# RWKV-7 chunk inverses: 16x16 diagonal blocks doubled twice, in place of 32x32 blocks doubled once

## The chip, the cores and the metric

The kernel runs on one core of a Trainium2 chip. The metric is the device time of one execution in microseconds (us), lower is better. Before the change three runs took 1123.34, 1129.8 and 1132.21 us; the median is 1129.8.

## The reference

One decoder layer on 512 tokens of width 1024, in float32. The token-mixing half computes one projection of the normed input, and from it two branches: an RWKV-7 scan over 16 heads of size 64, and a causal convolution of width 31 on 1024 channels. Both are gated, joined and projected back. A dense feed-forward half of width 4096 follows. The part that the change touches is the scan:

```
def step(S, inp):
    r_t, w_t, k_t, v_t, a_t, b_t = inp
    sa = jnp.einsum('bhij,bhj->bhi', S, a_t)
    S = S * w_t[:, :, None, :] + sa[..., None] * b_t[:, :, None, :] + v_t[..., None] * k_t[:, :, None, :]
    return S, jnp.einsum('bhij,bhj->bhi', S, r_t)
```

Taken over a chunk of 64 tokens, the steps inside the chunk depend on one another through a strictly lower triangular 64x64 matrix (per head and chunk). The kernel multiplies by the inverse of one minus that matrix, and so handles a chunk with a few matrix products in place of 64 steps.

## The kernel before, in words

The layer runs as one program on the five engines: PE (matrix products), DVE and POOL (vector work), ACT (activations and copies), SP (issues the DMAs). Large products are done as three passes over a high and a low part of each operand; the split of a weight tile into these parts is done on ACT and on DVE or POOL (`split`, L145), and a tile of raw weights is loaded for each projection (`wcol`, L154).

The 16 heads are handled in four quarters of four heads, that is, two pairs of heads each; a sequence of 512 tokens has 8 chunks, so a quarter has 32 chunk matrices. For a quarter these steps follow one another:

- R (`rkv_pair`, L483): projections for a pair of heads and their elementwise preparation.
- I (`products`, L547): PE forms the chunk matrices, DVE masks them into M (L567). Then DMAs write blocks of M to DRAM (L571): per pair the two diagonal 32x32 blocks and the off-diagonal one.
- V (`solve`, L580): reads the 64 diagonal 32x32 blocks of the quarter back into U (L586), two partitions to a block, one for the even and one for the odd rows of the inverse. POOL prepares X as the identity (L590, L593). 31 steps follow, each a product (L598) and a sum (L600) on DVE, each step depending on the one before. X is written to DRAM (L603).
- O (`scan_operands`, L606): transposes for the scan.
- M (`merge_inverses`, L629): reads the inverted blocks and the off-diagonal block into W (L639) and the diagonal blocks into RT (L640, L641). One transpose (L642), one product of 32x32 blocks on PE (L648), a copy (L650), a second product and four copies into RT (L652) give the off-diagonal block of the 64x64 inverse: left inverse times block times right inverse, for 32 matrices.
- S (`scan`, L655): the chunks of the quarter in order. For each chunk PE makes a first product that does not need the inverse (L669), one with the inverse RT (L680, recorded as L184), and the products for output and next state (L691, L693), with small copies on ACT and DVE between them.
- Y (`group_norm`, L707): normalises the output of the quarter.

The other steps of this phase are U and T (the convolution: projections, L732, and 30 taps per tile of 128 channels on DVE, L745), G and B (gates), N, and after the last quarter the tail (`enter_tail`, L822) with the output projection and then the feed-forward layer.

What sets the order of the work is the string ORDER (L35): it lists these steps, each with a number that lets its instructions go ahead of that many others in priority. A planner at build time orders the instructions of every engine by priority and by its own cost for each; on the chip each engine then works through its list in order, waiting on semaphores. All DMAs are issued by SP, in one list. U and W share one buffer of 4 KB per partition (tag "U" of the pool xq); X, and the scan's operands, are in the pool qp, which is closed before the tail.

Of the kernel before, what the change touches and what calls it, by code (L numbers as in the profile page):

```python
# [62 lines left out]
def tile_rwkv7_conformer(  # L63
# [389 lines left out]
    with ExitStack() as c1:  # L453
# [93 lines left out]
        def products(q, prs):  # L547

            d1 = dram.tile([3, 32, 32, 32], F32, name=f"d1_{q}")
            pcq[q] = qp.tile([C, NCHK, 4, 1], F32, tag="pcq", name=f"pcq{q}", bufs=2)  # L550
            for pr, d in enumerate(prs):
# [18 lines left out]
                for b, (s0, t0) in enumerate(((0, 0), (32, 32), (0, 32))):  # L570
                    nc.sync.dma_start(out=d1[b, pr * 16:(pr + 1) * 16].rearrange("h s t -> s h t"),  # L571
                                      in_=Mf[s0:s0 + 32, :, t0:t0 + 32])
# [5 lines left out]
            return d1  # L578

        def solve(q, d1):  # L580

            d2 = dram.tile([2, 32, 32, 32], F32, name=f"d2_{q}")
            U = xq.tile([P, 32, 32], F32, tag="U", name=f"U{q}")
            d1f = d1[0:2].rearrange("b h s t -> (b h) (s t)")
            for par in range(2):
                nc.sync.dma_start(out=U[64 * par:64 * par + 64].rearrange("p s t -> p (s t)"), in_=d1f)  # L586

            X = qp.tile([P, 16, 32], F32, tag="X", name=f"X{q}")
            tmp = qp.tile([P, 136], F32, tag="tmp", name=f"tmp{q}")
            G.memset(X, 0.0)  # L590
            for par in (0, 1):
                xv = X[64 * par:64 * par + 64]
                G.affine_select(out=xv, in_=xv, compare_op=ALU.not_equal, fill=1.0, base=-par,  # L593
                                pattern=[[-2, 16], [1, 32]], channel_multiplier=0)
            for s in range(31):
                n, m = s // 2 + 1, 31 - s
                tv = tmp[:, 0:n * m].rearrange("p (a b) -> p a b", b=m)
                V.tensor_tensor(tv, X[:, 0:n, s:s + 1].to_broadcast([P, n, m]),  # L598
                                U[:, s:s + 1, s + 1:32].to_broadcast([P, n, m]), op=ALU.mult)
                V.tensor_tensor(X[:, 0:n, s + 1:32], X[:, 0:n, s + 1:32], tv, op=ALU.add)  # L600
            d2v = d2.rearrange("b h (i two) t -> two (b h) i t", two=2)
            for par in range(2):
                nc.sync.dma_start(out=d2v[par], in_=X[64 * par:64 * par + 64])  # L603
            return d1, d2
# [24 lines left out]
        def merge_inverses(q, d1, d2):  # L629
# [4 lines left out]
            W = xq.tile([P, 4, 8, 32], F32, tag="U", name=f"W{q}")  # L634
            lay, grp = "h i t -> i h t", "(g x) i t -> g i x t"
            for g in range(4):
                gs = slice(32 * g, 32 * g + 32)
                for m, src in enumerate((d1[2], d2[0], d2[1])):
                    nc.sync.dma_start(out=W[gs, m], in_=src[8 * g:8 * g + 8].rearrange(lay))  # L639
            nc.sync.dma_start(out=RT[64:96, :, 0:32], in_=d2[0].rearrange(lay))  # L640
            nc.sync.dma_start(out=RT[96:128, :, 32:64], in_=d2[1].rearrange(lay))  # L641
            V.transpose(W[:, 3].rearrange("p x t -> p (x t)"), W[:, 1].rearrange("p x t -> p (x t)"))  # L642
            for a, b, dst in ((0, 3, 1), (1, 2, None)):
                px = pq.tile([P, 8, 32], F32, tag="q", name=f"px{q}{a}")
                for x_ in range(8):
                    for g in range(4):
                        gs = slice(32 * g, 32 * g + 32)
                        PE.matmul(px[gs, x_, :], W[gs, a, x_], W[gs, b, x_], start=True, stop=True)  # L648
                if dst is not None:
                    S.copy(W[:, dst], px)  # L650
# [459 lines left out]
```

## Time and profile before

| what | value |
|---|---|
| median of three runs | 1129.8 us |
| the profiled execution's own time | 1131.94 us |
| its span | 1130.2 us |
| PE busy | 1023.5 us, 91% of the span |
| DVE busy | 790.1 us, 70% |
| ACT busy | 479.1 us, 42% |
| POOL busy | 198.2 us, 18% |
| mean granted PE clock over the span | 0.953 of full speed |

An engine counts as busy while one of its instructions runs; matrix products overlap, so a busy PE is not a PE at its peak. The span is that of the profiled execution, and the time beside it is what the same execution took as a whole. The order of the phases in the span: until about 60 us input, norm and modulation, until about 600 us the projections, the scan and the convolution, until about 780 us the output projection and its surroundings, and then the feed-forward layer.

### The profile page before, as it was taken

Reading aid. Unit: us, or ns where it says so; the run is one execution under the profiler, and the core shown is the slowest. Engines: PE = TensorE matmul, PEld = TensorE weight load, DVE = VectorE, ACT = ScalarE, POOL = GpSimd, SP = SyncE. Lnnn points to the kernel's source line nnn. Section 1 sums busy time; section 2 is a strip of 40 time slices with the busy share of each in tenths; the row PEclk is TensorE's granted clock in tenths of the full one; section 3 lists DMA queues with packets and bytes.
Section 4 is the critical chain, followed back from the end, with each engine's and each line's share of the span. In section 5 each row is a group of like instructions: output and inputs, shape, how many; then the busy total and the mean of one; then the engine's idle time right before and its main releaser. Section 6 shows DMA issues by size and latency. Waiting matters only on the chain.

```text
span 1130.2 us, 16757 instructions
## 1 busy us (share of the span) xinstructions
PE 1023.5 (91%) x6037; PEld 792.5 (70%) x6037; DVE 790.1 (70%) x1622; ACT 479.1 (42%) x912; POOL 198.2 (18%) x191
## 2 busy tenths in 40 slices
PE   2999889889899789996997999899999999999995
PEld 1777666656677666665665767688888888888874
DVE  3859999969958997989455787585445445445557
ACT  5546445374644356534343433264323323423432
POOL 1123042222422533221121121200000000000002
PEclk9999999989999989996798999999999999999998
DMA  9622332331343234324257686731223323333332
GB/s 313 181 72 87 88 100 73 54 92 48 104 117 94 86 95 83 85 66 110 94 162 234 224 273 217 232 104 38 84 93 95 101 94 94 95 93 100 96 103 74
DMA packets 184605, 131.34 MB, mean 116 GB/s; under 512 B 49945, under 2 KB 152779, under 8 KB 184523
## 3 DMA queue, kind: packets, MB, share of 16 engines
q1 hardware_dynamic: 184523, 130.28, 39.1%
q8 instruction: 47, 0.77, 0.3%
q14 instruction: 35, 0.29, 0.1%
HBM read 116.61 MB, written 13.63 MB: 115 GB/s over the span
## 4 chain that ended last, share of the span: by engine, by line
PE 43%; DVE 16%; DMA 5%; issue 3%; ACT 3%; POOL 1%; SPq 0%; DVEq 0%; ACTq 0%; POOLq 0%
PE ps_fi L174 5%; PE ps_fi L175 5%; PE ps_fi L176 5%; DVE cz L745 5%; PE acc_fo L1005 4%; PE acc_fo L1004 4%; PE acc_fo L1003 4%; DMA ar<-in_ada_w_dram 2%; DVE tmp L598 1%; DVE aacc L217 1%; PE ps_ga L175 1%; PE ps_ga L176 1%; PE ps_ga L174 1%; DVE X L600 1%; PE pr L669 1%
## 5 line engine op out<-in xcount | busy, mean ns | idle before, releaser
L745 DVE SCALAR_TENSOR_TENSOR cz<-gl,cw,cz 128x512 f32<-128x512 f32 x240 | 200.8, 837 | 3.9 <-ACT cz L743 1.2
L151 DVE TENSOR_TENSOR lo_fo<-raw_fo,hi_fo 128x512 fp32r<-128x512 f32 x64 | 44.2, 691 | 92.1 <-ACT hi_fo L150 91.9
L175 PE MATMUL ps_fi<-hl,hi_fi 128*128 128x512 f32 (+1 forms) x288 | 105.6, 367 | 0.0
L176 PE MATMUL ps_fi<-hh,lo_fi 128*128 128x512 f32 (+1 forms) x288 | 105.3, 367 | 0.0
L174 PE MATMUL ps_fi<-hh,hi_fi 128*128 128x512 f32 (+1 forms) x288 | 105.0, 367 | 0.0
L1003 PE MATMUL acc_fo<-hi_fo,fh 128*128 128x512 f32 x256 | 101.3, 396 | 0.8 <-DVE t_fo L1010 0.8
L1004 PE MATMUL acc_fo<-lo_fo,fh 128*128 128x512 f32 x256 | 101.2, 395 | 0.0
L1005 PE MATMUL acc_fo<-hi_fo,fl 128*128 128x512 f32 x256 | 101.2, 395 | 0.0
L150 ACT CAST hi_fo<-raw_fo 128x512 fp32r<-128x512 f32 x64 | 39.7, 621 | 110.6 <-PE acc_fo L1005 87.8
L151 DVE TENSOR_TENSOR lo_fi<-raw_fi,hi_fi 128x512 fp32r<-128x512 f32 x64 | 43.8, 690 | 52.1 <-ACT hi_fi L150 51.2
L150 ACT CAST hi_fi<-raw_fi 128x512 fp32r<-128x512 f32 x64 | 39.9, 623 | 74.0 <-PE ps_fi L175 45.6
L1021 POOL TENSOR_TENSOR x<-x,fgain 128x512 f32<-128x512 f32 x4 | 5.5, 1392 | 363.8 <-ACT sq L1015 363.8
L175 PEld LDWEIGHTS ps_fi<-hl,hi_fi 128*128 128x128 f32 x288 | 54.3, 189 | 8.9 <-DVE hl L928 0.4
L176 PEld LDWEIGHTS ps_fi<-hh,lo_fi 128*128 128x128 f32 x288 | 54.3, 189 | 8.7
L174 PEld LDWEIGHTS ps_fi<-hh,hi_fi 128*128 128x128 f32 x288 | 54.0, 189 | 8.8 <-ACT hh L927 0.2
L174 PE MATMUL ps_u<-hh,hi_u 128*128 128x512 f32 x128 | 54.1, 422 | 5.4 <-DVE tr L466 2.9
L937 PE MATMUL acc_wo<-lo_wo,mh 128*128 128x512 f32 x128 | 53.0, 414 | 5.9 <-DVE lo_wo L151 3.2
L217 DVE SCALAR_TENSOR_TENSOR aacc<-ar,cact,aacc 128x512 f32<-128x512 f32 x56 | 49.9, 891 | 11.3 <-DMA ar<-in_ada_w_dram 10.7
L1003 PEld LDWEIGHTS acc_fo<-hi_fo,fh 128*128 128x128 f32 x256 | 48.2, 188 | 12.7 <-DVE t_fo L1010 1.3
L1005 PEld LDWEIGHTS acc_fo<-hi_fo,fl 128*128 128x128 f32 x256 | 48.2, 188 | 11.5
L1004 PEld LDWEIGHTS acc_fo<-lo_fo,fh 128*128 128x128 f32 x256 | 48.2, 188 | 11.5
L176 PE MATMUL ps_u<-hh,lo_u 128*128 128x512 f32 x128 | 54.9, 429 | 0.6 <-POOL Pt L512 0.6
(334 smaller groups left out, 2554.3 us busy)
## 6 DMA issues: line engine op xcount, KB each, us to landing
ar<-in_ada_w_dram SPq DMA_DIRECT2D x64, 256.0 KB
raw_fi<-in_w_ff_in_dram SPq DMA_DIRECT2D x64, 256.0 KB
raw_fo<-in_w_ff_out_dram SPq DMA_DIRECT2D x64, 256.0 KB
araw<-in_ada_w_dram SPq DMA_DIRECT2D x8, 1024.0 KB
raw_u<-in_w_in_dram SPq DMA_DIRECT2D x32, 256.0 KB
raw_wo<-in_w_out_dram SPq DMA_DIRECT2D x32, 256.0 KB
raw_k<-in_w_in_dram SPq DMA_DIRECT2D x16, 256.0 KB
raw_v<-in_w_in_dram SPq DMA_DIRECT2D x16, 256.0 KB
```

The source lines that it names most:

```text
L150: S.copy(hi, raw)
L151: (eng or V).tensor_tensor(lo, raw, hi.bitcast(F32), op=ALU.subtract)
L174: PE.matmul(ps[:, ts_], wh[:, i, :], mh[:, k, ts_], start=first, stop=False, skip_group_check=True)
L175: PE.matmul(ps[:, ts_], wh[:, i, :], ml[:, k, ts_], start=False, stop=False, skip_group_check=True)
L176: return PE.matmul(ps[:, ts_], wl[:, i, :], mh[:, k, ts_], start=False, stop=(k == KT - 1), skip_group_check=True)
L217: eng.scalar_tensor_tensor(acc, a, cact[:, k:k + 1], acc, op0=ALU.mult, op1=ALU.add)
L598: V.tensor_tensor(tv, X[:, 0:n, s:s + 1].to_broadcast([P, n, m]), U[:, s:s + 1, s + 1:32].to_broadcast([P, n, m]), op=ALU.mult)
L745: V.scalar_tensor_tensor(cz, gl[:, w:w + T], cw[:, w * KT + j:w * KT + j + 1], cz, op0=ALU.mult, op1=ALU.add)
L937: PE.matmul(wacc[h][tt], mh[k][:, ts_], wl, start=False, stop=False)
L1003: PE.matmul(acc[tt], fh[:, k, ts_], wh, start=(n == 0), stop=False)
L1004: PE.matmul(acc[tt], fh[:, k, ts_], wl, start=False, stop=False)
L1005: PE.matmul(acc[tt], fl[:, k, ts_], wh, start=False, stop=(n == KT - 1))
```

## The change

`products` writes seven blocks per pair in place of three: the four diagonal 16x16 blocks (dg), the two 16x16 blocks beside them (n16) and the 32x32 off-diagonal block (n32). `solve` has one block to a partition: 4 x 32 blocks of 16x16 fill 128 partitions, and the loop has 15 steps. U moves to the pool qp with a tag of its own, and one DMA reads it; one DMA writes X. `merge_inverses` zeroes half of a wider W (7 KB per partition), reads the 16x16 inverses into the diagonal places of 32x32 blocks, doubles them to inverted 32x32 blocks by two products and an addition on DVE, and doubles these as before. The diagonal blocks go to RT by eight ACT copies, where two DMAs did so before.

```diff
@@ -546,7 +546,9 @@
 
         def products(q, prs):
 
-            d1 = dram.tile([3, 32, 32, 32], F32, name=f"d1_{q}")
+            dg = dram.tile([4, 32, 16, 16], F32, name=f"dg_{q}")
+            n16 = dram.tile([2, 32, 16, 16], F32, name=f"n16_{q}")
+            n32 = dram.tile([32, 32, 32], F32, name=f"n32_{q}")
             pcq[q] = qp.tile([C, NCHK, 4, 1], F32, tag="pcq", name=f"pcq{q}", bufs=2)
             for pr, d in enumerate(prs):
                 j, AR, BK = d["j"], d["AR"], d["BK"]
@@ -567,40 +569,34 @@
                         freed = V.tensor_tensor(M[:, 4 * c4:4 * c4 + 4, e, :], pA[e],
                                                 mask.unsqueeze(1).to_broadcast([P, 4, P]), op=ALU.mult).ins
                 Mf = M.rearrange("p c h n -> p (c h) n")
-                for b, (s0, t0) in enumerate(((0, 0), (32, 32), (0, 32))):
-                    nc.sync.dma_start(out=d1[b, pr * 16:(pr + 1) * 16].rearrange("h s t -> s h t"),
-                                      in_=Mf[s0:s0 + 32, :, t0:t0 + 32])
+                hs = slice(pr * 16, (pr + 1) * 16)
+                for dst, s0, t0, n in [(dg[b], 16 * b, 16 * b, 16) for b in range(4)] + [
+                        (n16[0], 0, 16, 16), (n16[1], 32, 48, 16), (n32, 0, 32, 32)]:
+                    nc.sync.dma_start(out=dst[hs].rearrange("h s t -> s h t"), in_=Mf[s0:s0 + n, :, t0:t0 + n])
                 for e in range(2):
                     S.copy(M[0:64, :, e, 0:C], AR[64 * e:64 * e + 64, :, 0:C])
                     G.tensor_copy(pcq[q][:, :, 2 * pr + e, :], d["pc"][64 * e:64 * e + 64])
 
                 S.copy(AR[0:64, :, 0:C], AR[64:128, :, C:P])
-            return d1
+            return dg, n16, n32
 
         def solve(q, d1):
 
-            d2 = dram.tile([2, 32, 32, 32], F32, name=f"d2_{q}")
-            U = xq.tile([P, 32, 32], F32, tag="U", name=f"U{q}")
-            d1f = d1[0:2].rearrange("b h s t -> (b h) (s t)")
-            for par in range(2):
-                nc.sync.dma_start(out=U[64 * par:64 * par + 64].rearrange("p s t -> p (s t)"), in_=d1f)
-
-            X = qp.tile([P, 16, 32], F32, tag="X", name=f"X{q}")
-            tmp = qp.tile([P, 136], F32, tag="tmp", name=f"tmp{q}")
+            d2 = dram.tile([4, 32, 16, 16], F32, name=f"d2_{q}")
+            U = qp.tile([P, 16, 16], F32, tag="Us", name=f"U{q}")
+            nc.sync.dma_start(out=U.rearrange("p s t -> p (s t)"), in_=d1[0].rearrange("b h s t -> (b h) (s t)"))
+            X = qp.tile([P, 16, 16], F32, tag="X", name=f"X{q}")
+            tmp = qp.tile([P, 64], F32, tag="tmp", name=f"tmp{q}")
             G.memset(X, 0.0)
-            for par in (0, 1):
-                xv = X[64 * par:64 * par + 64]
-                G.affine_select(out=xv, in_=xv, compare_op=ALU.not_equal, fill=1.0, base=-par,
-                                pattern=[[-2, 16], [1, 32]], channel_multiplier=0)
-            for s in range(31):
-                n, m = s // 2 + 1, 31 - s
+            G.affine_select(out=X, in_=X, compare_op=ALU.not_equal, fill=1.0, base=0,
+                            pattern=[[-1, 16], [1, 16]], channel_multiplier=0)
+            for s in range(15):
+                n, m = s + 1, 15 - s
                 tv = tmp[:, 0:n * m].rearrange("p (a b) -> p a b", b=m)
                 V.tensor_tensor(tv, X[:, 0:n, s:s + 1].to_broadcast([P, n, m]),
-                                U[:, s:s + 1, s + 1:32].to_broadcast([P, n, m]), op=ALU.mult)
-                V.tensor_tensor(X[:, 0:n, s + 1:32], X[:, 0:n, s + 1:32], tv, op=ALU.add)
-            d2v = d2.rearrange("b h (i two) t -> two (b h) i t", two=2)
-            for par in range(2):
-                nc.sync.dma_start(out=d2v[par], in_=X[64 * par:64 * par + 64])
+                                U[:, s:s + 1, s + 1:16].to_broadcast([P, n, m]), op=ALU.mult)
+                V.tensor_tensor(X[:, 0:n, s + 1:16], X[:, 0:n, s + 1:16], tv, op=ALU.add)
+            nc.sync.dma_start(out=d2.rearrange("b h s t -> (b h) (s t)"), in_=X.rearrange("p s t -> p (s t)"))
             return d1, d2
 
         def scan_operands(q, prs):
@@ -631,23 +627,44 @@
 
             RT = xq.tile([P, 32, C], F32, tag="RT", name=f"RT{q}", bufs=2)
             G.memset(RT[96:128, :, 0:32], 0.0)
-            W = xq.tile([P, 4, 8, 32], F32, tag="U", name=f"W{q}")
-            lay, grp = "h i t -> i h t", "(g x) i t -> g i x t"
+            W = xq.tile([P, 7, 8, 32], F32, tag="U", name=f"W{q}")
+            L, N, Y, N2 = W[:, 0:2], W[:, 2:4], W[:, 4:6], W[:, 6]
+            G.memset(W[:, 0:4], 0.0)
+            lay = "h i t -> i h t"
             for g in range(4):
-                gs = slice(32 * g, 32 * g + 32)
-                for m, src in enumerate((d1[2], d2[0], d2[1])):
-                    nc.sync.dma_start(out=W[gs, m], in_=src[8 * g:8 * g + 8].rearrange(lay))
-            nc.sync.dma_start(out=RT[64:96, :, 0:32], in_=d2[0].rearrange(lay))
-            nc.sync.dma_start(out=RT[96:128, :, 32:64], in_=d2[1].rearrange(lay))
-            V.transpose(W[:, 3].rearrange("p x t -> p (x t)"), W[:, 1].rearrange("p x t -> p (x t)"))
-            for a, b, dst in ((0, 3, 1), (1, 2, None)):
-                px = pq.tile([P, 8, 32], F32, tag="q", name=f"px{q}{a}")
-                for x_ in range(8):
+                hs = slice(8 * g, 8 * g + 8)
+                for b in range(4):
+                    r, c = 32 * g + 16 * (b % 2), 16 * (b % 2)
+                    nc.sync.dma_start(out=L[r:r + 16, b // 2, :, c:c + 16], in_=d2[b, hs].rearrange(lay))
+                for b in range(2):
+                    nc.sync.dma_start(out=N[32 * g:32 * g + 16, b, :, 16:32], in_=d1[1][b, hs].rearrange(lay))
+                nc.sync.dma_start(out=N2[32 * g:32 * g + 32], in_=d1[2][hs].rearrange(lay))
+
+            def blocks(a, b, n, nm):
+
+                px = pq.tile([P, n, 32], F32, tag="q", name=f"px{q}{nm}")
+                for x_ in range(n):
                     for g in range(4):
                         gs = slice(32 * g, 32 * g + 32)
-                        PE.matmul(px[gs, x_, :], W[gs, a, x_], W[gs, b, x_], start=True, stop=True)
-                if dst is not None:
-                    S.copy(W[:, dst], px)
+                        PE.matmul(px[gs, x_, :], a[gs, x_], b[gs, x_], start=True, stop=True)
+                return px
+
+            def flat(t_):
+                return t_.rearrange("p b h t -> p (b h) t")
+
+            V.transpose(Y.rearrange("p b h t -> p (b h t)"), L.rearrange("p b h t -> p (b h t)"))
+            px = blocks(flat(N), flat(Y), 16, "a")
+            S.copy(flat(Y), px)
+            px = blocks(flat(Y), flat(L), 16, "b")
+            V.tensor_tensor(flat(L), flat(L), px, op=ALU.add)
+            V.transpose(Y[:, 0].rearrange("p h t -> p (h t)"), L[:, 0].rearrange("p h t -> p (h t)"))
+            px = blocks(N2, Y[:, 0], 8, "c")
+            S.copy(Y[:, 1], px)
+            px = blocks(Y[:, 1], L[:, 1], 8, "d")
+            for g in range(4):
+                gs, hs = slice(32 * g, 32 * g + 32), slice(8 * g, 8 * g + 8)
+                S.copy(RT[64:96, hs, 0:32], L[gs, 0])
+                S.copy(RT[96:128, hs, 32:64], L[gs, 1])
             for g in range(4):
                 S.copy(RT[64:96, 8 * g:8 * g + 8, 32:64], px[32 * g:32 * g + 32])
             return RT
```

## Rows read from the trace of the kernel before

**Rows 1.** Stretches: us, busy us per engine, granted PE clock, DMA share, GB/s.

```profile
230.00:330.00 100.00, 90.33 (x780) 65.90 (x780) 75.01 (x191) 54.36 (x109) 29.67 (x30) 0.95 0.34 89
...
440.00:540.00 100.00, 86.09 (x893) 62.88 (x892) 89.69 (x215) 46.41 (x107) 19.66 (x14) 0.88 0.36 93
540.00:600.00 60.00, 58.48 (x432) 41.89 (x431) 28.86 (x88) 26.09 (x56) 10.35 (x8) 0.91 0.40 131
140.00:540.00 400.00, 353.49 (x2790) 261.53 (x2789) 351.20 (x779) 196.09 (x394) 122.53 (x110) 0.92 0.34 87
```

**Rows 2.** Chain of waits, 440 to 540 us, shares of the stretch.

```profile
by line: DVE cz L745 33.7%; DVE X L600 6.0%; DVE tmp L598 6.0%; PE px L648 4.3%; PE pr L669 3.6%; issue 3.4%; PE psa L184 3.2%; PE pn L691 3.2%; PE pA L184 3.1%; PE ps_ga L174 2.6%; PE ps_ga L175 2.6%; ACT RT L652 2.5%; PE pyt L724 1.9%; DV
```

**Rows 3.** Timeline of PE: start, us, instructions, idle before and its releaser.

```profile
511.32 0.68 PE L669 MATMUL pr<-RV,M 64*64 64x64 f32 x8
...
531.74 1.45 PE L184 MATMUL psa<-Rs,RT 64*64 64x64 f32 x8 [0.47 <-ACT RT L652]
```

**Rows 4.** Groups by line, 140 to 540 us: busy us, mean ns, idle.

```profile
L598 DVE TENSOR_TENSOR tmp<-X,U 128x126 f32<-128x126 f32 (+22 forms) x124 | 47.5, 383 | 0.8
...
L600 DVE TENSOR_TENSOR X<-X,tmp 128x126 f32<-128x126 f32 (+22 forms) x124 | 40.1, 323 | 0.9
```

**Rows 5.** Groups by line and form, the solve's two lines.

```profile
L600 DVE TENSOR_TENSOR X<-X,tmp 128x30 f32<-128x30 f32 x8 | 1.4, 178 | 0.0
...
L600 DVE TENSOR_TENSOR X<-X,tmp 128x70 f32<-128x70 f32 x4 | 0.9, 225 | 0.1
...
L598 DVE TENSOR_TENSOR tmp<-X,U 128x45 f32<-128x45 f32 x4 | 0.8, 193 | 0.0
...
L598 DVE TENSOR_TENSOR tmp<-X,U 128x16 f32<-128x16 f32 x4 | 0.7, 172 | 0.0
```

**Rows 6.** Timeline of all engines, 490 to 500 us.

```profile
494.60 1.34 POOL L151 TENSOR_TENSOR lo_gb<-raw_gb,hi_gb 128x512 fp32r<-128x512 f32 x1 [1.13 <-ACT hi_gb L150]
...
494.84 1.24 DVE L598 TENSOR_TENSOR tmp<-X,U 128x130 f32<-128x130 f32 x1
```

**Rows 7.** Timeline, 214 to 226 us, the first merge and PE's next products.

```profile
218.35 0.44 DVE L642 STREAM_TRANSPOSE W<-W 128x256 f32<-128x256 f32 x1
...
218.84 0.88 PE L648 MATMUL px<-W 32*32 32x32 f32 x64 [2.59 <-DVE W L642]
...
219.76 0.37 ACT L650 COPY W<-px 128x256 f32<-128x256 f32 x1 [5.41 <-PE px L648]
...
221.23 1.08 PE L648 MATMUL px<-W 32*32 32x32 f32 x64
...
222.24 0.70 PE L176 MATMUL ps_k<-hh,lo_k 128*128 128x512 f32 x1
...
222.38 1.49 ACT L652 COPY RT<-px 32x256 f32<-32x256 f32 x4 [2.24 <-PE px L648]
...
223.25 0.39 PE L176 MATMUL ps_k<-hh,lo_k 128*128 128x512 f32 x1
```

**Rows 8.** Groups by line, 140 to 540 us, other prices.

```profile
L648 PE MATMUL px<-W 32*32 32x32 f32 x512 | 8.7, 212 | 3.4 <-DVE W L642 2.6 <-ACT W L650 0.5 <-issue 0.3
...
L541 DVE TENSOR_TENSOR bo<-pb,tv 128x512 f32<-128x512 f32 x6 | 4.1, 689 | 4.6 <-PE pb L539 4.6
...
L590 POOL MEMSET X<- 128x512 f32 x3 | 1.6, 521 | 19.2 <-DMA d<-X 19.2
```

**Rows 9.** Timeline of SP, issues of the last quarter's solve and merge.

```profile
457.21 1.13 SPq L586 DMA_DIRECT2D U<-d  x2
...
509.22 1.26 SPq L603 DMA_DIRECT2D d<-X  x2
510.53 8.20 SPq L639 DMA_DIRECT2D W<-d  x12
```

**Rows 10.** Timeline of DVE, first and last instruction of the last solve.

```profile
468.82 0.18 DVE L598 TENSOR_TENSOR tmp<-X,U 128x31 f32<-128x31 f32 x1
...
507.89 1.30 DVE L600 TENSOR_TENSOR X<-X,tmp 128x16 f32<-128x16 f32 x1
```

## The prediction

> **What bounds the kernel now.** I read the table of stretches first. From 140 to 540 us, the part in which the solves and merges lie, PE is busy 353.5 us of 400 and DVE 351.2, at a mean granted PE clock of 0.92: two engines at 88%, each held up by the other [rows 1]. Where DVE is less loaded, PE is denser: 90.3% in the stretch with DVE at 75.0%, 97.5% (58.48 of 60) where DVE has 28.86 of 60. From 440 to 540, DVE at 89.69 goes with PE at 86.09 and a clock of 0.88.
>
> The chain of waits from 440 to 540 then says which engine leads there: 33.7% is the convolution's DVE taps, 12.0% the solve's two DVE lines, and the merge shows as 4.3% PE and 2.5% ACT [rows 2]. The timeline names what waits for it. The first product of the last quarter's scan, which needs no inverse, runs at 511.32; the next, which needs it, at 531.74, released by the ACT copy that ends the merge [rows 3]. So the last scan stands ready for some 20 us: its inverse is late, and DVE is full while it is made.
>
> **The solve.** Before, 124 products and 124 sums take 47.5 + 40.1 = 87.6 us [rows 4]. The new loop issues 15 of each per quarter, 120 in all, on 15 to 64 elements ((s+1)(15-s)). Undisturbed instructions of near sizes take 172 ns at 16 elements, 178 at 30, 193 at 45 and 225 at 70 [rows 5]; on a line through these the fifteen sizes add up to 3.0 us (0.156 us each, and 0.98 ns for each of 680 elements), so 6.0 us per quarter with products and sums, 24.1 us in all. The old 248 on the same line (31 sizes, 2856 elements) would be 61.2; the other 26.4 us is stall. Such a stall is in the rows: a 130-element product takes 1.24 us from 494.84 and ends where a POOL subtraction (494.60 to 495.94) ends [rows 6].
>
> If all stalls go, DVE saves 87.6 - 24.1 = 63.5 us. If each moves to the DVE instruction that comes next, 61.2 - 24.1 = 37.1. I take the stall per instruction (26.4/248 = 0.107 us) on 120, so 24.1 + 12.8 = 36.9 and a saving of 50.7. The Trainium skill (SBUF — State Buffer, "SBUF: two separate sides") has GpSimd instructions and Vector instructions with two SBUF inputs lock each other out for a whole instruction; the row agrees, and as the taps have two such inputs as well, the saving would by that rule be the 37.1.
>
> **The merge, per quarter.** Now, in the first quarter, it runs from the transpose at 218.35 to the last copy at 223.87, 5.5 us: transpose 0.44, product 0.88, copy 0.37, product 1.08, four copies 1.49, sum 4.26, and 1.26 of gaps over four hand-overs, 0.31 each [rows 7]. After: a 512-wide transpose (twice 0.44 = 0.87), a 16-head product (1.76), a 512-wide copy (twice 0.37 = 0.74), a 16-head product (2.16), an add from PSUM (0.69), transpose 0.44, product 0.88, copy 0.37, product 1.08, copies 1.49 [rows 7, 8]: 10.5, and nine hand-overs at 0.31, 2.8. That is 13.3, or 7.8 longer. With no gaps it would be 10.5 (+5.0).
>
> On the engines: PE has 512 records now, 8.7 us [rows 8], and 1,536 after, 26.1: +17.4 (+14 at the 0.88/64 of one group). The matmul behind a merge product takes 0.70 instead of 0.39 [rows 7], so eight more groups add some 2.5 to 3. The Trainium skill (TensorEngine Tiling (Array Packing), Key Properties) says that a change of tiling mode drains TensorE, a rule against this change; the row agrees in sign. DVE gets 0.43 + 0.69 + 0.44 more per quarter, 6.2 in all, so its net saving is 44.5 us (31 to 57). ACT gets 32 more copies at 0.37 and wider ones, about 15 us, in a stage where it has 196 of 400 [rows 1]; eight of the twelve copies need only the diagonal blocks, so they lie beside the last two products. If ACT is not free there, they cost 8 x 0.37 = 3 us on the path. POOL fills W with zeros, 1,024 wide, twice the 0.52 of the 512-wide fill [rows 8], and X is half as wide with one select less: about even, and W's fill waits no longer for the solve, since U has a buffer of its own. If W's fill is late, it costs 1.0.
>
> **The queue and the DMAs.** 44 transfers per quarter replace 24: 14 for 6 from M, 1 for 2 into U, 1 for 2 out of X, 28 for 14 into W and RT. On SP twelve loads of the last merge take 8.20 us, 0.68 each, behind a 1.26 us write of X [rows 9]. Sixteen of the new loads wait for X: 16 x 0.68 = 10.9 plus 0.63 for one write, against 9.5 plus two loads into RT: I take +1. The twelve that need only M can go ahead; if the planner leaves them behind, +8.2. The last pair's write of M has four more issues ahead of U, 2.7 us: taken at nothing, because U's two transfers, issued from 457.21 on, were 10 us ahead of the solve's first instruction at 468.82 (DVE taps lay between) [rows 9, 10], and at 2.7 if that cover goes. Weight loads stand behind all of these on SP; they wait for buffers anyhow. The runs of 64 bytes are no row of this trace: none to +3 us per quarter, the latter being as much again as one group of four loads. The Trainium skill (DMA: Bandwidth & Descriptors, Specifications) puts line rate at 512 bytes or more, with a read-modify-write below, which speaks for the +3.
>
> **The sum.** Path of the last quarter: its solve goes from 468.82 to 509.19 with other DVE work between, 62 instructions at 0.65 us [rows 10]; 30 at that pitch take 19.5, so -20.9. With +7.8 and +1 the inverse is ready 12 us earlier, and the scan that waits for it can use that; with all upper bounds (+8.2 in place of +1, +2.7, +3, +3, +1.0) it is 5 us later.
>
> Check by engines: PE's 353.5 + 17.4 + 3 = 374. If the clock goes from 0.92 to the 0.95 of the stretch from 230 to 330, that is 374 x 0.92/0.95 = 362, and at a density between the 90.3% and 97.5% of rows 1, 93.5%, the stage takes 387 instead of 400. DVE's 351 - 44.5 = 307 fits easily: PE is late next. Both give 12 to 13. The profiled execution took 1131.9 (span 1130.2 and 1.7 around it), 2.1 above the median of 1129.8: 1131.9 - 12 - 2 = **1118 us**.
>
> **The rivals.**
> - **PE keeps its density.** At 90.3% the 362 us need 401: no gain, 1130. For it: PE's clock and its waits come from many places. Against: the scan that stands from 511 to 531.
> - **DVE was the whole cause.** The stage goes at the 97.5% of the stretch from 540 to 600: 362/0.975 = 371, 29 us less, 1101. For it: DVE at 307 of 371 is still less than 88%. Against: scans are chains of small steps that no engine's relief shortens.
> - **Slower: the merge's hops in PE's queue.** PE works in order, and four dependent products per quarter stand in it, with scans and projections behind. If each of nine hand-overs costs the 2.59 that PE waited for the transpose in the first quarter [rows 7], the merge takes 10.5 + 23.3 = 33.8, 28 more; with loads at +8.2 and the solve at -20.9 the last inverse comes 15 later: 1145. It decides from a merge of about 25 us on (18 with loads at +8.2). For it: instructions are ordered by a planner that sees only its own costs, and the priorities in the order string count on the old lengths.
>
> **Chances.** Forecast 0.48, with a range of its own of 1108 to 1128; full relief 0.15; no change 0.15; slower 0.22. Within 1%, about what a measurement can tell from no change, is 1118.5 to 1141. Half of the forecast's share lies below that: 0.25 + 0.15 = 0.40 faster; 0.23 + 0.15 = 0.38 the same; 0.22 slower. For 8 in 10 the range takes about half of either outer case: 1102 to 1145.
>
> **What would show it.** The solve's two lines at 120 together and 30 to 42 us; DVE busy 40 to 50 us less up to 540; merge records three times as many, 24 to 28 us; from the wide transpose to the last copy 11 to 15 us; the last scan's second product within 10 us of its first; a clock above 0.92. I am wrong if the solve ends no earlier although it is shorter, if merges stretch past 20 us, or if PE's idle time moves to another wait (the group norm's transposes, the weight splits) and stays at 46 us.

## The result: slower by 1.5%, and the profile after

The changed kernel takes 1143.92 us (median of four runs, 1141.16 to 1145.85) against 1126.57 for the kernel before in the same rounds: a ratio of 1.0148, 95% interval 1.0111 to 1.0185. Forecast was 1118, so the change went the other way. Three executions that came out slow (two of held_packed below, one of the kernel before) are left out of all times.

The first two parts of the page of the changed kernel (busy us, share of the span, instructions):

```profile
span 1144.1 us, 18874 instructions
...
PE 1039.9 (91%) x7061; PEld 803.6 (70%) x7061; DVE 756.5 (66%) x1502; ACT 495.1 (43%) x948; POOL 196.8 (17%) x191
```

DVE has 33.6 us less than before and PE 16.4 more. The span less PE's busy time, which is PE's idle time, is 104.2 us, and was 106.7. So PE's busy time grew by more than the 13.9 us of span, and of idle time only 2.5 us went. The stretches that answer to [rows 1], same columns:

```profile
440.00:540.00 100.00, 95.00 (x898) 66.20 (x899) 67.38 (x164) 47.08 (x100) 23.04 (x16) 0.97 0.26 66
540.00:600.00 60.00, 54.67 (x556) 40.86 (x557) 40.36 (x113) 27.64 (x65) 8.11 (x6) 0.89 0.35 112
140.00:540.00 400.00, 363.46 (x3646) 265.94 (x3648) 301.95 (x627) 206.13 (x413) 118.65 (x108) 0.94 0.28 74
```

Until 540 us PE is a little denser (90.9% for 88.4%) and DVE has 49.2 us less, both as meant; from 540 to 600 PE has lost 3.8 us. The solve's two lines, which answer to [rows 4] (busy us, mean ns, idle):

```profile
L596 DVE TENSOR_TENSOR tmp<-X,U 128x15 f32<-128x15 f32 (+7 forms) x60 | 18.8, 313 | 0.4
L598 DVE TENSOR_TENSOR X<-X,tmp 128x15 f32<-128x15 f32 (+7 forms) x60 | 18.5, 308 | 0.4
```

The first merge on the timeline, for [rows 7] (start, us, instructions, idle before and its releaser):

```profile
187.28 0.70 DVE L655 STREAM_TRANSPOSE W<-W 128x512 f32<-128x512 f32 x1
...
190.39 1.29 PE L649 MATMUL px0a<-W 32*32 32x32 f32 x128
191.72 0.59 ACT L657 COPY W<-px0a 128x512 f32<-128x512 f32 x1 [0.79 <-PE px0a L649]
...
192.36 1.77 PE L649 MATMUL px0b<-W 32*32 32x32 f32 x100
...
194.80 0.51 PE L649 MATMUL px0b<-W 32*32 32x32 f32 x28 [0.68 <-issue]
195.35 0.69 DVE L659 TENSOR_TENSOR W<-W,px0b 128x512 f32<-128x512 f32 x1 [3.56 <-PE px0b L649]
...
202.16 1.49 ACT L669 COPY RT<-px0d 32x256 f32<-32x256 f32 x4
```

It takes 16.4 us, from 187.28 to 203.65; the second and third take 15.5 and 15.9, the last 19.6 (shown further below). (A float32 product of 32x32 is two records on PE, so a doubling's 64 products show as x128.) Last, what answers to [rows 10] and [rows 3], the last solve on DVE and the last scan on PE:

```profile
479.45 0.16 DVE L596 TENSOR_TENSOR tmp<-X,U 128x15 f32<-128x15 f32 x1
...
506.58 0.17 DVE L598 TENSOR_TENSOR X<-X,tmp 128x15 f32<-128x15 f32 x1
```

```profile
524.17 0.68 PE L686 MATMUL pr<-RV,M 64*64 64x64 f32 x8
...
544.92 0.44 PE L184 MATMUL psa<-Rs,RT 64*64 64x64 f32 x4 [0.67 <-ACT RT L669]
```

The last solve is half as long in instructions and ends at 506.75, before at 509.19. The scan's first product with the inverse comes at 544.92, 13.2 us later than before, where 12 earlier was forecast.

### The profile page after: what moved, and what is told of

The parts are those of the page before. It is cut to its first block, busy times and chain, and to the rows that moved or that the text cites. A ratio compares the mean times of both kernels' runs of the same rounds, so it can differ in the third digit from the quotient of the medians.

```text
span 1144.1 us, 18874 instructions
## 1 busy us (share of the span) xinstructions
PE 1039.9 (91%) x7061; PEld 803.6 (70%) x7061; DVE 756.5 (66%) x1502; ACT 495.1 (43%) x948; POOL 196.8 (17%) x191
## 4 chain that ended last, share of the span: by engine, by line
PE 47%; DVE 9%; DMA 7%; issue 4%; ACT 3%; POOL 1%; SPq 0%; DVEq 0%; ACTq 0%; POOLq 0%
PE ps_fi L174 5%; PE ps_fi L175 5%; PE ps_fi L176 5%; PE acc_fo L1022 4%; PE acc_fo L1020 4%; PE acc_fo L1021 4%; DMA ar<-in_ada_w_dram 3%; DVE cz L762 2%; DVE aacc L217 1%; PE ps_u L175 1%; PE ps_u L174 1%; PE ps_u L176 1%; PE pr L686 1%; PE pn L708 1%; PE psa L184 1%
## 5 line engine op out<-in xcount | busy, mean ns | idle before, releaser
L217 DVE SCALAR_TENSOR_TENSOR aacc<-ar,cact,aacc 128x512 f32<-128x512 f32 x56 | 48.9, 873 | 13.8 <-DMA ar<-in_ada_w_dram 13.2
```

Source lines behind the costliest of these rows:

```text
L217: eng.scalar_tensor_tensor(acc, a, cact[:, k:k + 1], acc, op0=ALU.mult, op1=ALU.add)
```

## The experiments

Three theories. **A:** PE's work sets the time, and DVE's relief is worth nothing. **B:** the relief is worth what was forecast, and the doubling takes more back than it was charged with. **C:** each edit makes the planner order everything anew, and the order string fits the old kernel alone. Medians are in us, each with the ratio to before and its interval; before lies between 1128.7 and 1130.3 in all rounds of experiments.

### In the planner's own order

**half_solve**, the kernel before with half of the solve's steps left out:

```diff
-            for s in range(31):
+            for s in range(15):
```

> The kernel before with the solve's loop cut to its first 15 steps of 31 (the rest of the inverse is left out): about 47 us less DVE work, merge, DMAs and PE work as before. Theory A (the time follows PE's work, and DVE was not the limit): within 5 us of before. Theory B (DVE's relief is worth what I forecast and the merge takes more back): 10 to 20 us faster. Theory C (every edit changes the planner's order, and the order string fits only the old one): 5 to 17 us slower although it only leaves work out.

Measured: 1138.19, 1.0078 [1.0040, 1.0116]. Work left out, and slower: neither A nor B has that, C does.

**old_solve_new_products**, the kernel before with the doubling on top, on the old operands:

```diff
+            V.transpose(Y.rearrange("p b h t -> p (b h t)"), L.rearrange("p b h t -> p (b h t)"))
+            px = blocks(flat(L), flat(Y), 16, "a")
+            S.copy(flat(Y), px)
+            px = blocks(flat(Y), flat(L), 16, "b")
+            V.tensor_tensor(flat(L), flat(L), px, op=ALU.add)
```

> The kernel before, old solve and old DMAs, with the doubling's two 16-head products, wide transpose, wide copy and addition put into the merge (its operands are the old ones, so the inverse is not the right one). Theory A: 13 to 17 us slower, as the changed kernel is. Theory B: 20 to 28 us slower, since nothing is given back. Theory C: anywhere from 5 to 17 us slower, and no nearer to the PE work added than the other kernels are.

Measured: 1153.32, 1.0223 [1.0164, 1.0281].

**after_no_doubling**, the changed kernel without those five lines:

> The changed kernel with the doubling left out of the merge (the first wide transpose, two 16-head products, copy, addition): short solve, new DMAs and the twelve copies stay. Theory A: 0 to 4 us above before, the added PE work being gone. Theory B: 8 to 15 us faster than before. Theory C: 5 us or more slower than before.

Measured: 1126.51, 0.9987 [0.9959, 1.0015]. Against the changed kernel's 1.0148 the doubling is the loss; the shorter solve seems worth nothing, as in A.

**order_nudge**, the kernel before with three priorities of the order string raised by one (the unchanged steps between them are left out here):

```diff
-R1:0v ... I3:1000 V3:1000
+R1:1v ... I3:1001 V3:1001
```

> The kernel before with three priorities in the order string moved by one (R1:0 to 1, I3 and V3 from 1000 to 1001): the same instructions, planned in another order. Theories A and B: within 4 us of before. Theory C: 5 us or more slower.

Measured: 1175.45, 1.0423 [1.0367, 1.0478]. The same instructions take 46 us more. So a difference of 10 or 20 us between two kernels can come from the plan alone, and the three runs above prove neither A nor B. PE's waits from 140 to 600 us show where it went (waiter, releaser, us in total, times, longest):

```profile
PE pA L184 <- DVE M L567: 18.9, 8, 12.8
PE pb L539 <- DVE tr L537: 16.3, 4, 6.8
PE ps_gb L174 <- DVE gl L738: 7.7, 1, 7.7
```

The chunk products wait 12.8 us at one place for a mask that DVE has late in its list; in the kernel before the first of these is 0.7.

**before_new_numbers** and **after_old_numbers** ask whether it is the numbers: a step's priority counts the instructions ahead of it, and a quarter of the changed kernel counts 126 more. Each step gets the number it has in the other kernel:

```diff
-            with ahead(int(hp.rstrip("v"))):
+            with ahead(int(hp.rstrip("v")) + tc.cur_priority - number):
```

> The kernel before, instruction for instruction, but every step starts at the priority number that it has in the changed kernel (a step's number counts the instructions ahead of it, and a quarter of the changed kernel counts 126 more). If the shift of the numbers alone makes the plan worse, the time goes most of the way to the changed kernel's: 1138 to 1150 us. If the cost lies in the new work (the products on PE or the hand-overs of the merge), it stays at the time of before, 1122 to 1133.

Measured: 1127.06, 0.9996 [0.9968, 1.0024].

> The changed kernel, instruction for instruction, but every step starts at the priority number that it has in the kernel before. If the shift of the numbers is the cost, the time falls to that of before or below: 1115 to 1130 us. If the work is the cost, 1138 to 1150.

Measured: 1157.81, 1.0267 [1.0214, 1.0319]. The shift of the numbers costs the kernel before nothing, and taking it back makes the changed kernel worse. That leaves the new work, as the planner costs it, as what moves the plan; no run shows that by itself.

**products_off_chain** and **hops_only** take the doubling apart on the kernel before:

```diff
+            for nm in "ab":
+                py = pq.tile([P, 16, 32], F32, tag="q", name=f"py{q}{nm}")
+                for x_ in range(16):
+                    for g in range(4):
+                        gs = slice(32 * g, 32 * g + 32)
+                        PE.matmul(py[gs, x_, :], W[gs, 0, x_ % 8], W[gs, 0, x_ % 8], start=True, stop=True)
```

> The kernel before, with the doubling's 128 products of 32x32 per quarter put ahead of the merge, on the off-diagonal block alone; nobody reads them and nothing waits for them, so no hand-over is added. If PE's own work is the cost (512 records more, 12.3 us in the changed kernel's trace, and the changes of mode around them): 1140 to 1150 us. If the hand-overs in the merge's chain are the cost: at most 5 more than before, 1124 to 1133.

Measured: 1156.24, 1.0249 [1.0195, 1.0303], above both ranges. (Its text speaks of 512 records: they are 512 products, 1,024 records.)

> The kernel before, with the doubling's chain (wide transpose, product, copy, product, addition) ahead of the old merge, each product on 4 records in place of 64, so that PE's work stays as it was and the hand-overs are there. If the hand-overs are the cost, most of the 25 us that the whole doubling added to this kernel comes: 1142 to 1153 us. If PE's own work is the cost: 1126 to 1135.

Measured: 1138.83, 1.0096 [1.0066, 1.0126], between the two theories. The order had moved in both, so they were no clean measure of price yet.

### In the old order, held

A plan can be held. Every instruction gets as its priority its place in the plan of the kernel before; new ones take the place of the merge's first transpose (loads and writes that of the load or write they stand for). In the traces the 5,525 records of PE outside the merge's products then stand, on average, 2 to 6 places from where they stood before when all quarters are edited, and 0.1 in held_half_3, which changes the last solve alone; in half_solve it was 41. Some single records still move by over a hundred places. Every instruction goes through one helper here, so the profile shows the helper's line for all of them; they are told apart by the names of their tiles.

```diff
+        def call(*a, **k):
+            with self.at():
+                return f(*a, **k)
...
+    def at():
+        return tc.high_priority(offset=tc.cur_priority - next(RANKS))
...
-    V, S, G, PE = nc.vector, nc.scalar, nc.gpsimd, nc.tensor
+    V, S, G, PE, SP = (Held(e, at) for e in (nc.vector, nc.scalar, nc.gpsimd, nc.tensor, nc.sync))
```

The edits of **held_half**, **held_new_products**, **held_after** and **held_no_doubling** are those of half_solve, old_solve_new_products, the change, and after_no_doubling.

> half_solve (15 of the 31 steps, the rest of the solve left out), but the order is held: every instruction has as its priority the place that it has in the plan of the kernel before, so that PE's list keeps nearly the old order (a mean shift of 3 places of 4265, 20 without it). If DVE's relief is worth what was forecast and only the new order ate it up: 1112 to 1122 us. If the relief is worth little even in the old order, because DVE does not set the pace: 1123 to 1131. The free half_solve was 1.0078 times before; if that was not the order, 1134 or more.

Measured: 1106.61, 0.9801 [0.9762, 0.9840].

> old_solve_new_products (the doubling's transposes, products, copy and addition ahead of the old merge, old solve) in the held order. If the doubling costs its work on PE alone, 12 to 17 us: 1138 to 1146. If its hand-overs stand in the merge's chain as well: 1147 to 1158, as without the hold. If the 25 us were mostly the order: under 1137.

Measured: 1156.31, 1.0211 [1.0147, 1.0276], in the range with the hand-overs; held_off_chain below reaches nearly that without any.

> The changed kernel, complete, in the held order (its new instructions of the merge stand where the merge's first transpose stood). If the change was right and the order string no longer fitted it, as the forecast's sum has it: 1110 to 1123 us. If the relief of DVE is worth little and the doubling costs its PE work: 1137 to 1147. If the hand-overs come on top: 1148 to 1160.

Measured: 1140.09, 1.0100 [1.0059, 1.0141], in the range for little relief, though the relief was not little.

> after_no_doubling (the changed kernel without the first of the two doublings: wide transpose, two products, copy, addition left out) in the held order. Its distance to held_after is the price of the doubling, to before the worth of the shorter solve. If the relief is worth the forecast's 12 to 20 us: 1107 to 1117 us. If little: 1120 to 1131.

Measured: 1114.94, 0.9884 [0.9837, 0.9930].

This is B, and A falls: with the order held the shorter solve is worth 23.4 us (1130.03 less 1106.61), more than was forecast, and 15.1 with what else the change brings along. Only half of it is idle time: held_half's page has

```profile
PE 1012.9 (91%) x6037; PEld 784.0 (71%) x6037; DVE 763.0 (69%) x1494; ACT 480.0 (43%) x912; POOL 198.2 (18%) x191
```

at a span of 1108.4 us, so PE idles 11.2 us less than before and is busy 10.6 us less with the very same products: from 60 to 780 us its mean granted clock is 0.95 in place of 0.93. The doubling costs 25.2 (1140.09 less 1114.94) or 26.3 (on the old solve). C is true beside it: in the planner's own order half_solve took 32 us longer than held_half, and after_no_doubling 12 us longer than held_no_doubling. Between the free changed kernel and held_after the intervals overlap. The pages of held_no_doubling and held_after:

```profile
span 1113.4 us, 16776 instructions
...
PE 1012.9 (91%) x6037; PEld 785.9 (71%) x6037; DVE 753.1 (68%) x1494; ACT 493.3 (44%) x944; POOL 194.2 (17%) x191
```

```profile
span 1139.0 us, 18833 instructions
...
PE 1037.7 (91%) x7061; PEld 803.7 (71%) x7061; DVE 760.7 (67%) x1502; ACT 496.4 (44%) x948; POOL 197.7 (17%) x191
```

The doubling adds 25.6 us of span and 24.8 of busy PE; what PE idles is 100.5 and 101.3. So it all shows as busy PE. Of the 24.8 the merge's products are 16.0 (22.8 us in held_after, 6.8 in held_no_doubling); the other 9 are other products that take longer, some 4 of them the chunk products (pA).

**held_off_chain**, the doubling's records without a hand-over behind them:

> products_off_chain (the kernel before with the doubling's 512 records more than before's 512, read by nobody) in the held order. If the doubling's price of 25 us (held_new_products) is that of its records in PE's list: 1148 to 1158 us. If half of it is the hand-overs behind them: 1138 to 1146. If the records cost no more than their own 15 ns each: 1135 to 1140.

Measured: 1151.18, 1.0212 [1.0159, 1.0266]: 21 us for 512 products that nobody reads. That leaves the hand-overs some 5 of the 26 by the medians, and nothing by the ratios (1.0211 and 1.0212, each good to 0.6%). What the other 21 are made of shows on PE behind the third quarter's products (same columns as above):

```profile
451.93 1.93 PE L436 MATMUL py2a<-W 32*32 32x32 f32 x128
453.79 0.79 PE L436 MATMUL pA<-AR,BK 64*128 64x128 f32 x2
454.51 0.93 PE L436 MATMUL py2b<-W 32*32 32x32 f32 x51
456.26 0.86 PE L436 MATMUL py2b<-W 32*32 32x32 f32 x77 [0.82 <-issue]
...
461.09 0.49 PE L436 MATMUL pA<-AR,BK 64*128 64x128 f32 x5 [2.42 <-issue]
...
463.62 2.06 PE L436 MATMUL pA<-AR,BK 64*128 64x128 f32 x16
```

The same sixteen chunk products in the kernel before:

```profile
444.26 1.16 PE L184 MATMUL pA<-AR,BK 64*128 64x128 f32 x16
```

And the 20 us from some 3 us ahead of these products on, held_off_chain and then before (columns of [rows 1]):

```profile
448.00:468.00 20.00, 14.89 (x433) 10.87 (x431) 8.14 (x15) 5.79 (x15) 0.96 (x1) 0.83 0.23 68
```

```profile
437.00:457.00 20.00, 18.39 (x246) 13.49 (x245) 14.88 (x24) 12.31 (x32) 1.29 (x1) 1.00 0.35 86
```

Three things: the products' own 3.7 us; chunk products beside them that take 2.06 in place of 1.16, in a stretch with a granted clock of 0.83 in place of 1.00; and idle time ("issue") in which PE waits for no other engine and no transfer of data, 3.2 here. Over the kernel, from 60 to 780 us, that idle time is 11.0 us where before had 0.3; but PE's idle time as a whole is only 3.2 us longer than before (109.9 and 106.7), so most of the 11.0 stands where PE would have waited for something else.

The clock in these 20 us, held_off_chain (same columns):

```profile
452.00:455.00 3.00, 3.00 (x166) 2.71 (x170) 0.69 (x1) 0.00 (x0) 0.00 (x0) 0.50 0.47 160
456.00:462.00 6.00, 3.32 (x156) 2.77 (x156) 0.39 (x1) 1.41 (x5) 0.00 (x0) 1.00 0.36 104
463.00:465.00 2.00, 2.00 (x31) 1.77 (x32) 0.50 (x1) 0.53 (x2) 0.00 (x0) 0.50 0.00 0
```

It stands at 0.50, the lower of its two levels (1.2 GHz), twice. Shortly before the first fall PE idled 1.87 us (until 450.87, for a DVE result), before the second 2.42 us (until 461.09, "issue"). So here the clock falls after PE idled; that small products lower it by themselves is not shown.

What "issue" stands for can be read from the DMA queues. The page counts a queue that carries instructions, before and in held_off_chain (packets, MB, share of 16 engines):

```profile
q8 instruction: 47, 0.77, 0.3%
```

```profile
q8 instruction: 55, 0.90, 0.3%
```

Eight packets more, of 16,384 bytes each, go with 2,048 PE instructions more (1,024 product records and as many weight loads): one packet to 256 instructions. Counting PE's instructions in the trace from 0, the eight "issue" waits of held_off_chain end at the instructions 2241, 2497, 4289, 4545, 6337, 6593, 8385 and 8641, all a multiple of 256 apart, and each ends 1.3 to 1.5 us after such a packet has landed; the 2.42 us wait ends at 461.09, its packet ran from 458.53 to 459.66. The four of the changed kernel end at numbers of the same row (1985, 4289, 6593 and 8385), 1.3 to 1.6 us after a packet. So PE waits there for its own next 256 instructions. A group of 128 records and its weight loads use up as many in 1.3 us.

**held_packed** does the doubling with half the products: the two 16x16 blocks of a chunk side by side in one 32x32 operand, N and R block diagonal, and copies and additions half as wide.

```diff
+            V.transpose(flat(Y), L[:, :, :, 0:16].rearrange("p b h t -> p h b t"))
+            px = blocks(N, Y, 8, "a")
+            S.copy(N, px)
+            px = blocks(N, R, 8, "b")
+            V.tensor_tensor(L[:, :, :, 16:32], L[:, :, :, 16:32], px.rearrange("p h (b t) -> p b h t", b=2), op=ALU.add)
```

> The changed kernel with a packed doubling: the two 16x16 blocks of a chunk stand side by side in one 32x32 operand (right inverses and off-diagonal blocks as block diagonals), so that each product has 32 records per quarter in place of 64, on 256-wide copies and additions; in the held order; complete. If the price of the doubling goes with its records, half of 25 us is saved against held_after (1140): 1125 to 1131 us. If it goes with the hand-overs, which are as many as before: 1135 to 1141. The order of the transfers is that of held_after with 8 loads more per quarter.

Measured: 1124.1, 0.9959 [0.9929, 0.9989]: 16 us under held_after, with as many hand-overs, though 256-wide ones. With held_off_chain that says that the price goes with the products in the main; what the narrower copies and addition save was not measured apart.

**held_packed_3** has the packed change in the last quarter alone, **held_half_3** the cut solve there alone:

```diff
-                scans[i] = solve(i, scans[i])
+                scans[i] = (solve16 if i in NEW else solve)(i, scans[i])
```

```diff
-            for s in range(31):
+            for s in range(15 if q == 3 else 31):
```

> The kernel before with the packed change in the last quarter alone, in the held order (mean shift in PE's list 0.3 places); complete. If the last quarter's path sets the end, as the forecast had it, and a packed doubling costs it 3 us of PE and some 4 of hand-overs: 1115 to 1123 us. If the gain lies in all quarters alike, a quarter of the relief less a quarter of the price is nothing: 1126 to 1132. If the longer merge at the end decides: over 1134.

Measured: 1124.72, 0.9968 [0.9942, 0.9994], between two of the ranges.

> The kernel before with 15 of the 31 solve steps in the last quarter alone (the rest of that solve left out), in the held order. If the last quarter's path sets the end, as the forecast had it (its solve 20.9 us shorter, the scan behind it earlier by that): 1108 to 1116 us, most of held_half's 23 us. If the relief counts in every quarter alike: 1122 to 1127. If it counts only where DVE is fullest, in the stretches up to 440 us: 1127 to 1132.

Measured: 1124.45, 0.9943 [0.9919, 0.9968]: 5.9 us by the medians, 6.4 by the ratio, about a quarter of held_half's 23.4. The last quarter counts for its share and no more. Here the forecast's path can be read undisturbed, DVE and then PE:

```profile
468.81 0.18 DVE L413 TENSOR_TENSOR tmp<-X,U 128x31 f32<-128x31 f32 x1
...
487.63 0.29 DVE L413 TENSOR_TENSOR X<-X,tmp 128x136 f32<-128x136 f32 x1
...
507.76 0.67 PE L413 MATMUL pr<-RV,M 64*64 64x64 f32 x8
...
518.95 0.44 PE L413 MATMUL psa<-Rs,RT 64*64 64x64 f32 x4
```

The solve ends 21.3 us earlier (20.9 was forecast) and the scan's product with the inverse starts 12.8 earlier. The end comes 6 earlier.

**held_packed_013** has the packed change in three quarters:

```diff
+NEW = (0, 1, 3)
```

> The packed change in the first, second and last quarter, the third as in the kernel before, in the held order; complete. If each quarter's gain is its relief less the price of its products, and the third quarter has none: 1117 to 1123 us. If the gains of single quarters don't add (held_packed and held_packed_3 both stand at 1125): 1123 to 1128. If mixing old and new solves upsets the order on DVE: over 1130.

Measured: 1119.84, 0.9914 [0.9880, 0.9947]. It is the whole layer, and faster than before by 10 us (10.5 by the medians, 9.7 by the ratio). The packed change in one, three and four quarters gives 0.3%, 0.9% and 0.4%, so the quarters do not share alike: the third seems to lose something, though the last two intervals overlap.

## Why the prediction was wrong, point by point

- **The solve: right.** 36.9 us were forecast, 18.8 + 18.5 = 37.3 came. The stall per instruction stayed; DVE's 49.2 us less until 540 us are at the upper end of the 40 to 50 named.
- **The merge: too low, most of all where it counted.** 13.3 us were forecast; the four take 16.4, 15.5, 15.9 and 19.6, with more time between the steps than the 0.31 us a hand-over that was charged. The records on PE were put at 26.1 us and are 21.
- **The path of the last quarter, the step that carried the 12 us: wrong, and charged with too little.** Read from [rows 3], a scan that stands ready for 20 us looked like 20 us to be had. But PE did other work in that time: in the kernel before, 507 to 532 us has

```profile
507.00:532.00 25.00, 16.69 (x196) 12.41 (x195) 24.68 (x51) 10.53 (x27) 3.91 (x3) 0.75 0.46 107
```

  PE busy for 16.69 us. Work that filled that time is then missing elsewhere: in held_half_3 the idle time stands behind the scan, where 560 to 600 us has

```profile
560.00:600.00 40.00, 32.09 (x195) 23.71 (x189) 19.68 (x48) 18.20 (x39) 9.51 (x7) 0.93 0.48 153
```

  32.09 us of PE, in place of 38.58 before, and so 12.8 us of earlier start were worth some 6. And the changed kernel never got the earlier start. Its last solve begins 10.6 us later than before (479.45 for 468.82) and is 13.1 us shorter, not 20.9, so it ends 2.4 earlier: the planner filled the room on DVE with convolution taps. In the stretch of the last solve, 479.4 to 506.8 us in the changed kernel and 468.8 to 509.2 before, they are (min/median/max ns, first and last start):

```profile
L762 DVE SCALAR_TENSOR_TENSOR cz<-gl,cw,cz x23: 708/742/1664, 478.8 to 506.7; 128x512 f32<-128x512 f32 x23
```

```profile
L745 DVE SCALAR_TENSOR_TENSOR cz<-gl,cw,cz x16: 735/740/1652, 467.2 to 507.2; 128x512 f32<-128x512 f32 x16
```

  The prediction took "30 at that pitch" for the old mix of steps and taps; the mix is the planner's to choose, and it chose 23 taps for 30 instructions in place of 16 for 62. From the end of the solve to the merge's first transpose it is 19.6 us, before 16.8 (+1 was forecast; the write of X leaves SP 4.2 us after the solve). And the last merge takes 19.6 us where before took 6.9, so 12.7 more in place of 7.8, and 4.45 of them PE waits for instructions. First and last step of the last merge before, and then of that in the changed kernel:

```profile
525.95 0.44 DVE L642 STREAM_TRANSPOSE W<-W 128x256 f32<-128x256 f32 x1
531.33 1.51 ACT L652 COPY RT<-px 32x256 f32<-32x256 f32 x4 [2.72 <-PE px L648]
```

```profile
526.39 0.70 DVE L655 STREAM_TRANSPOSE W<-W 128x512 f32<-128x512 f32 x1
...
529.53 1.33 PE L649 MATMUL px3b<-W 32*32 32x32 f32 x102
...
535.31 0.58 PE L649 MATMUL px3b<-W 32*32 32x32 f32 x26 [4.45 <-issue]
...
544.51 1.51 ACT L669 COPY RT<-px3d 32x256 f32<-32x256 f32 x4
```

  So the step that failed is the sum's last one, that an inverse ready earlier in the last quarter brings the end forward by as much, with the doubling charged once, as 7.8 us of that quarter's merge. In the held order the doubling costs PE's list 25.2 us over all quarters, more than the 15.1 that the rest of the change gains.
- **The check by engines: nearly the right term, outvoted.** It had 17.4 + 3 us more work for PE, and 24.8 is what the doubling adds in the held order. It then let a better clock (0.95) and a density of 93.5% pay for it twice over. In the changed kernel the clock of that stretch came to 0.94 and the density to 90.9%. The 93.5% was chosen between two rows without a reason, so that both ways gave 12 to 13 us was no confirmation.
- **The mode changes.** Forecast was 2.5 to 3 us for the whole kernel beyond the products' own time; in the held order some 9 of the 24.8 are beyond it. The Trainium skill (TensorEngine Tiling (Array Packing), Key Properties) has a change of mode drain TensorE. That agrees in sign (behind px3a the first 128x512 product takes 0.50 us, the next 0.40), but no run here separates a drain from the clock and the waits for instructions.
- **The rivals.** The slower one forecast 1145, and 1143.9 came. Its last inverse was to be 15 us later, and the scan's product that waits for it came 13.2 later. But it has the hand-overs as the cost, with merges of 34 us and late loads, and the merges take up to 19.6 and held_off_chain leaves the hand-overs 5 us of the doubling's 26 or less. So its number came in the main by luck. Its last remark, that the priorities count on the old lengths, is not it either: the old numbers brought 1157.8. "PE keeps its density" came nearest in mechanism (90.9% for 90.3%), and lacks the price beside the products.
- **Transfers.** No sign of the 64-byte runs: DMA's share until 540 us fell from 0.34 to 0.28, and no wait of PE on a load of W appears among the larger ones.

Open: how the 9 us beyond the products split between the clock, the waits for instructions and a change of mode, since no run changes one of these alone; whether and why the third quarter's packed merge loses; and what the hand-overs cost alone in the held order, which was not run.

## What to carry to other kernels

Where two engines are both near full, charge what an edit adds to the second one in full, at its measured price with the neighbours' included, and don't pay for it with a density that is only hoped for. A step that "stands ready" is worth only the time in which its engine idles meanwhile: look at the engine's busy share there before you count it. Where a planner orders the work, hold the order before you price an edit: here three priorities moved by one cost 46 us, and the same cut of the solve made the kernel 8 us slower in a free order and 23 us faster in a held one. And count instructions beside elements: products so small that 256 PE instructions pass in 1.3 us can outrun the loading of the next ones.

## What the runs showed of the hardware

- Many small products in a row cost PE more than their records: 512 products of 32x32 with no reader took 21 us, 41 ns each, where their records take some 27 (held_off_chain, 13.7 us busy in eight groups).
- PE's instructions come in packets of 16,384 bytes, 256 instructions each (55 for 47 with 2,048 PE instructions more). PE waited for them in and behind groups of small products, 11.0 us from 60 to 780 us in held_off_chain and 6.7 in the changed kernel, each time until 1.3 to 1.6 us after a packet had landed (before had 0.3 us of idle time called "issue"); the longest wait, 4.45 us, cuts a group of the last merge in two.
- PE's busy time is no fixed sum for fixed products: held_half has the products of before and 10.6 us less of it, at a granted clock of 0.95 in place of 0.93 from 60 to 780 us.
